# Phase 1 of a bidirectional RWKV-7 and short-convolution layer: TensorE's order written out by hand in the recurrence's groups

## The chip, the cores and the metric

The kernel runs on one core of one Trainium2 chip. The metric is the device time of one execution in microseconds (us). The time given for a kernel is the median of its runs; before the change it is 1721.12 us (three runs, 1720.58 to 1724.52).

## What is computed

One layer on 2176 tokens (128 context tokens, then 2048 latent tokens in rows of 64) of width 1024. Cut to what matters here (the heads are 64 wide, `d` is the direction of the scan):

```python
h = rmsnorm(x) * (1 + scale) + shift
r, k, v, g_a, b_gate, c_gate, u_conv, g_b = split(h @ w_in)      # 8 x 512 columns
r, k, v = token_shift(r, k, v)                                   # neighbours in a row, mixed by mu
w[d] = w0[d] + tanh(h @ decay_down[d]) @ decay_up[d]             # "lora": 64 wide
decay[d] = exp(-exp(-softplus(-w[d]) - 0.5))
a[d] = sigmoid(iclr_bias[d] + (h @ iclr_down[d]) @ iclr_up[d])
kk = k * kk_scale;  kk = kk / norm_per_head(kk)
kd[d] = k * (1 + (a[d] - 1) * ka_scale)
y = scan(r, decay, kd, v, kk, a, both directions)                # phase 2
y = groupnorm(y) + sum_per_head(r * (kd[0] + kd[1]) * bonus_rk) * v
ya = y * silu(g_a);  yb = b_gate * conv3(c_gate * u_conv) * silu(g_b)
out = x + gate * (concat(ya, yb) @ w_out);  out = rmsnorm(out)
```

## The kernel before

Three phases follow each other. Phase 1 makes the projections and everything that the scan needs and spills it to scratch in HBM; phase 2 does the scan in chunks; phase 3 does the output projection. The change is in phase 1.

Phase 1 goes over the tokens in three thirds of two blocks each (`THIRD`, `BLK`): five blocks have 384 tokens, the last has 256. In a third the blocks' inputs `h` stay in SBUF. First `lora_down` projects both blocks onto the loras (four tiles `mml`, in PSUM). Then come the recurrence's groups: for each of four groups `g` of 128 channels and each block `j` of the third, `groupA(g, j, ...)`, which I call a unit, so eight units to a third. Then `groupB` does the convolution's groups in the same manner (`mmc`, `mmu`, `mmgb`, `mmb`).

`dense` is one projection of one unit, 24 matmuls of 128x128 by 384 columns (8 slices of the width, times three products of high and low parts, lines 158 to 160). In the order in which the program is written a unit is:

- `mmk`, the keys. `shifted` takes them from PSUM with two ScalarE operations (`rawl`, `q1k`), GpSimd adds the neighbours (`shk`, line 314), VectorE joins them (`ok`, line 320). ScalarE squares them (`sq`), and `part_sum` sums the squares per head: `parts_of` splits a tile into a high part (ScalarE, `hshs`, line 194) and a low part (GpSimd, `hsls`, line 195), and two matmuls with a matrix of ones sum both (`pss`, lines 202 and 203).
- `mmr`, the receptances, shifted alike (`or`).
- For each direction the two lora-ups (`up`, lines 355 and 356, eight matmuls to a unit), a tanh of each (ScalarE `t` and `ta`), a scan over the chunk (VectorE, lines 365 and 367), exponentials (`pp`), and four operands for phase 2, written on VectorE into a ring of four `sp` tiles and spilled (`al`, `rh`, `ka`, `be`, lines 377 to 392).
- The bonus: `kd` of both directions are added (line 396) and multiplied by `rS` (line 397; I call its result `bs`), and `part_sum` sums it per head: ScalarE `hshb`, GpSimd `hslb`, TensorE `psb`.
- `mmv`, the values, shifted (`ov`), transposed by three matmuls (`psv`, line 403), freed of their mean (`vmean`, `vt`, lines 412 and 413) and spilled from `vt` by a DMA on SP's queue (line 414).
- `mmg`, the gate (`sg`), and last `q`, which needs `psb`, `ov` and `sg`, spilled like the operands.

Three things bind these steps to each other. PSUM has five buffers for the projections and lora-ups (`pmm`) and three for the sums and transposes (`pax`). The low parts of both sums and the transposed values share one SBUF buffer: `lo` in `parts_of` and `vt` both have the tag `"vt"` with `bufs=1`, so the next low part can only be written when the values have left the buffer by their DMA. The high parts share one too (`"hsh"`), and the squares `sq` share theirs with `lf` of `lora_down`.

The order of the instructions on each engine is not the written one: a list scheduler with a timing model of its own sets it when the program is built, on all engines in phase 1. On the chip each engine then runs its list strictly in that order. (Phase 2 already has its main part under `tc.manual_schedule`, which keeps the written order on the engines that it names.) On TensorE the scheduler starts each unit before the one ahead is finished: `psb` and `psv` of a unit stand between the products of the next one.

Of the kernel before, what the change touches and what calls it, by code (L numbers as in the profile page):

```python
# [10 lines left out]
ALU = mybir.AluOpType  # L11
# [38 lines left out]
def phase1(K):  # L50
# [50 lines left out]
    def dcol(i):  # L101
        return dv[:, i:i + 1]
# [48 lines left out]
    def dense(w, hh, n, nm):  # L151
        ps = pmm.tile([128, 384], F32, tag="mm", name=f"mm{nm}_{K.u()}")
        products(ps, w, hh, n, range(8))
        return ps
# [43 lines left out]
    def part_sum(o, t_, n, nm, eng=G):  # L198

        hi, lo = parts_of(t_, n, nm, eng)  # L200
        ps = pax.tile([128, 384], F32, tag="ax", name=f"ps{nm}")
        T.matmul(ps[:, :n], o[:], hi[:, :n], start=True, stop=False)
        T.matmul(ps[:, :n], o[:], lo[:, :n], start=False, stop=True)
        return ps
# [123 lines left out]
    def groupA(g, j, ws, hh, lw, pre):  # L328
        t0, n = BLK[j]
# [2 lines left out]
        wk, wr_, wv, wg = ws  # L332
        psk, psr = pre or (None, None)

        kS = shifted(psk or dense(wk, hh, n, "k"), j, 1, g, "k", 1)
        sq = tl("sq")
        P.activation(sq[:, :n], kS[:, :n], AF.Square, scale=vcol(V_KK + g))
        pss = part_sum(onr, sq, n, f"s{g}_{j}")
# [4 lines left out]
        P.activation(kk[:, :n], kS[:, :n], AF.Identity, scale=vcol(V_KK + g))  # L343
        kkn = n2
        V.tensor_tensor(kkn[:, :n], kk[:, :n], n2[:, :n], ALU.mult)
        rS = shifted(psr or dense(wr_, hh, n, "r"), j, 0, g, "r", 1)
        kds = []
        for d in range(2):
            cs = slice(g * 128, g * 128 + 128)
# [45 lines left out]
        bs = kds[0]  # L395
        V.tensor_tensor(bs[:, :n], kds[0][:, :n], kds[1][:, :n], ALU.add)
        V.scalar_tensor_tensor(bs[:, :n], bs[:, :n], dcol(D_RKQ + g), rS[:, :n], ALU.mult, ALU.mult)
        psb = part_sum(onr, bs, n, f"b{g}_{j}")
        vS = shifted(dense(wv, hh, n, "v"), j, 2, g, "v", 1)

        psv = pax.tile([128, 3, 128], F32, tag="ax", name=f"psv{g}_{j}")
        for i in range(n // 128):
            T.transpose(psv[:, i, :], vS[:, i * 128:(i + 1) * 128], idt[:])
# [9 lines left out]
        V.scalar_tensor_tensor(heads(vt), mn[:, :m].unsqueeze(3).broadcast_to((128, m, 2, 64)), -1.0 / 64, heads(psv), ALU.mult, ALU.add)  # L413
        nc.sync.dma_start(S["vt"][t0:t0 + n, g * 128:(g + 1) * 128].rearrange("(a p) c -> p a c", p=128), vt[:, :n // 128])

        psg = dense(wg, hh, n, "g")
        tg = tl("sg", 2)
        P.activation(tg[:, :n], psg[:, :n], AF.Tanh, scale=0.5)
        sg = tg
        V.scalar_tensor_tensor(sg[:, :n], tg[:, :n], 1.0, psg[:, :n], ALU.add, ALU.mult)  # L420
        spill("sg", g, j, sg, "sg")
        q = tl("sp", 4)
        V.tensor_tensor(q[:, :n], psb[:, :n], vS[:, :n], ALU.mult)
        V.scalar_tensor_tensor(q[:, :n], q[:, :n], dcol(D_GBH + g), sg[:, :n], ALU.add, ALU.mult)
        spill("q", g, j, q, "q")

    def groupB(g, j, ws, hh):
        t0, n = BLK[j]
# [92 lines left out]


    up = {}

    def run(gen):
        for _ in gen:
# [17 lines left out]
    for t3, js in enumerate(THIRD):  # L544
        wd, wi = wlora if t3 == 0 else (load_w(32), load_w(33))
        lws = {}
        pre = {}
        for j in js:
            if j not in hs:
                if t3 == 0:  # L550
                    pre[0] = psf[2:]
                    ws = ws0 + [load_w(cb) for cb in (8, 12)]
                    nc.sync.dma_start(smask[:], A["cst"][:, 128:512])
                run(make_h(j, xb[j]))
            lws[j] = lora_down(j, wd, wi, psf[:2] if j == 0 else None)
        if t3 == 0:
            load_up()
        for g in range(4):
            if t3 or g:
                ws = [load_w(cb + g) for cb in (4, 0, 8, 12)]  # L560
            for j in js:
                groupA(g, j, ws, hs[j], lws[j], pre.pop(j, None))
        early = gate_rows() if t3 == 0 else iter(())
        if t3 == 2:
            for p in (pax, ta_, hr, ca):
                p.close()
            early = K.early()
        for g in range(4):
            ws = [load_w(cb + g) for cb in (20, 24, 28, 16)]
            for j in js:  # L570
                groupB(g, j, ws, hs[j])
                for _ in range(4 if t3 == 2 else 1):
                    next(early, None)
            if g == 1 and t3 < 2:
                j, j2 = THIRD[t3 + 1]
                run(make_h(j, norm(j, load_x(j))))
                xb[j2] = norm(j2, load_x(j2))
        for _ in early:
            pass
# [925 lines left out]
```

## Time and profile before

| | |
|---|---|
| median of three runs | 1721.12 us |
| the profiled execution | 1714.66 us, its span 1712.9 us |
| TensorE's mean granted clock | 0.957 |
| recurrence's groups, third 1 | 69.9 to 236.2 us of the span: 166.3 us |
| recurrence's groups, third 2 | 406.7 to 585.9 us: 179.2 us |
| recurrence's groups, third 3 | 736.9 to 880.3 us: 143.4 us |
| phase 2's first products | from 907.8 us |

The windows begin where TensorE has done the lora-downs and end where it begins the convolution's groups. Times of single rows are microseconds from the start of the span; a matmul's own duration is longer than the distance to the next, since they are pipelined, so a string of matmuls is measured from start to start. `[x <-Y]` behind a row of the timeline is the time that the engine stood idle ahead of it, and what ended that.

### The profile page before, as it was taken

Reading aid. Unit: us, or ns where it says so; the run is one execution under the profiler, and the core shown is the slowest. Engines: PE = TensorE matmul, PEld = TensorE weight load, DVE = VectorE, ACT = ScalarE, POOL = GpSimd, SP = SyncE. Lnnn points to the kernel's source line nnn. Section 1 sums busy time; section 2 is a strip of 40 time slices with the busy share of each in tenths; the row PEclk is TensorE's granted clock in tenths of the full one; section 3 lists DMA queues with packets and bytes.
Section 4 is the critical chain, followed back from the end, with each engine's and each line's share of the span. In section 5 each row is a group of like instructions: output and inputs, shape, how many; then the busy total and the mean of one; then the engine's idle time right before and its main releaser. Section 6 shows DMA issues by size and latency. Waiting matters only on the chain. (4 is left out here: it accounts for less than half of the span.)

```text
span 1712.9 us, 42020 instructions
## 1 busy us (share of the span) xinstructions
PE 1561.0 (91%) x17364; PEld 1432.1 (84%) x17364; DVE 1145.1 (67%) x2133; ACT 792.4 (46%) x1590; POOL 517.4 (30%) x951
## 2 busy tenths in 40 slices
PE   5999899999888999999999988888989898898998
PEld 2898899899788999989898987778878786776886
DVE  5988887544677736466884455788888885475333
ACT  4555554323444413145541135777768676422222
POOL 0022220000222200012214406676767675121221
PEclk7999999999999999999999988999999998799999
DMA  9688876674788835448876644556575744454342
GB/s 373 219 246 236 241 235 226 224 244 117 194 199 192 195 127 182 161 128 222 228 205 225 235 101 131 147 143 183 145 186 154 179 132 136 128 180 162 119 147 92
DMA packets 204271, 313.43 MB, mean 183 GB/s; under 512 B 58024, under 2 KB 147496, under 8 KB 190000
## 3 DMA queue, kind: packets, MB, share of 16 engines
q1 hardware_dynamic: 168496, 310.61, 60.0%
q10 hardware_dynamic: 35584, 0.14, 1.4%
q8 instruction: 136, 2.23, 0.6%
q14 instruction: 55, 0.45, 0.1%
HBM read 207.79 MB, written 102.91 MB: 181 GB/s over the span
## 5 line engine op out<-in xcount | busy, mean ns | idle before, releaser
L912 POOL TENSOR_TENSOR zt<-zt,ztmp 128x30 f32<-128x30 f32 (+7 forms) x510 | 201.6, 395 | 39.7
L909 POOL TENSOR_TENSOR ztmp<-ab,zt 128x60 f32<-128x60 f32 (+7 forms) x255 | 134.2, 526 | 129.5 <-DVE ab L900 110.9
L1048 PE MATMUL psS<-sv,E 128*64 128x64 f32 x2176 | 105.4, 233 | 16.3 <-DVE sv L1074 10.2
L1048 PEld LDWEIGHTS psS<-sv,E 128*64 128x64 f32 x2176 | 90.8, 144 | 31.4 <-issue 16.0
L314 POOL TENSOR_TENSOR shk<-rawl 128x384 f32<-128x384 f32 (+1 forms) x24 | 20.5, 854 | 276.8 <-ACT rawl L310 276.7
L1074 DVE TENSOR_TENSOR sv<-psS,pc 64x128 f32<-64x128 f32 x254 | 66.6, 278 | 55.3 <-PE psS L1048 54.0
L1022 DVE TENSOR_TENSOR E<-psE,msk 128x512 f32<-128x512 f32 x136 | 91.5, 680 | 17.5 <-PE psE L1017 16.8
L1003 ACT ACTIVATE stf<-psX 64x512 f32<-64x512 f32 x136 | 80.4, 591 | 32.9 <-PE psX L999 31.0
L158 PE MATMUL mmv<-h,w 128*128 128x384 f32 (+1 forms) x192 | 70.2, 366 | 19.7 <-ACT q1r L312 10.6
L1441 POOL TENSOR_TENSOR z<-z,x 128x512 f32<-128x512 f32 x32 | 41.1, 1288 | 149.8 <-DVE z L1437 121.1
L999 PE MATMUL psX<-F,zb 64*64 64x128 f32 x1088 | 52.0, 302 | 19.8 <-issue 11.8
L159 PE MATMUL mmv<-h,w 128*128 128x384 f32 (+1 forms) x192 | 68.1, 354 | 0.0
L160 PE MATMUL mmv<-h,w 128*128 128x384 f32 (+1 forms) x192 | 67.7, 353 | 0.1
L158 PE MATMUL mmg<-h,w 128*128 128x384 f32 (+1 forms) x192 | 63.4, 330 | 3.3 <-ACT rawc L317 1.6
L158 PE MATMUL mmc<-h,w 128*128 128x384 f32 (+1 forms) x192 | 64.2, 335 | 0.5 <-DMA w<-scr_wsp 0.5
L159 PE MATMUL mmc<-h,w 128*128 128x384 f32 (+1 forms) x192 | 63.1, 329 | 0.0
L158 PE MATMUL mmgb<-h,w 128*128 128x384 f32 (+1 forms) x192 | 63.1, 328 | 0.0
L160 PE MATMUL mmc<-h,w 128*128 128x384 f32 (+1 forms) x192 | 63.0, 328 | 0.0
L160 PE MATMUL mmb<-h,w 128*128 128x384 f32 (+1 forms) x192 | 62.9, 328 | 0.0
L159 PE MATMUL mmgb<-h,w 128*128 128x384 f32 (+1 forms) x192 | 62.9, 328 | 0.0
L195 POOL TENSOR_TENSOR hsls<-sq,hshs 128x384 fp32r<-128x384 f32 (+1 forms) x24 | 30.6, 1277 | 106.8 <-DMA scr_vt<-vt 41.9
L160 PE MATMUL mmgb<-h,w 128*128 128x384 f32 (+1 forms) x192 | 62.9, 327 | 0.0
(312 smaller groups left out, 5147.0 us busy)
## 6 DMA issues: line engine op xcount, KB each, us to landing
w<-scr_wsp SPq DMA_DIRECT2D x68, 1024.0 KB, 6.6
scr_wsp<-w SPq DMA_DIRECT2D x34, 1024.0 KB, 6.1
rr<-scr_ops SPq DMA_DIRECT2D x32, 1024.0 KB, 9.0
scr_ops<-sp SPq DMA_DIRECT2D x160, 192.0 KB, 5.3
wr<-in_win SPq DMA_DIRECT2D x34, 512.0 KB, 7.4
x<-in_x SPq DMA_DIRECT2D x17, 512.0 KB, 3.7
wadas<-in_wada SPq DMA_DIRECT2D x8, 1024.0 KB, 15.0
sv<-scr_vt SPq DMA_DIRECT2D x32, 256.0 KB, 3.7
```

The lines of the kernel that those rows point to most:

```text
L158: T.matmul(ps[:, :n], w[:, 0, k], hh[:, 0, k, :n], start=k == 0, stop=False)
L159: T.matmul(ps[:, :n], w[:, 0, k], hh[:, 1, k, :n], start=False, stop=False)
L160: T.matmul(ps[:, :n], w[:, 1, k], hh[:, 0, k, :n], start=False, stop=k == 7)
L195: eng.tensor_tensor(lo[:, :n], t_[:, :n], hi[:, :n].bitcast(F32), ALU.subtract)
L909: G.tensor_tensor(tv, ab[:, j:j + 2, j + 2:32].unsqueeze(1).broadcast_to((128, kn, 2, n)), zt[:, :kn, j:j + 2].unsqueeze(3).broadcast_to(( ...
L912: G.tensor_tensor(zt[:, :kn, j + 2:32], zt[:, :kn, j + 2:32], tv[:, :, r], ALU.subtract)
L999: T.matmul(px[e][hr_, a, :], B.zb[er, gi * 8 + hd * 4 + a, :], g.F[er, hd * 4 + a, :], start=True, stop=True)
L1003: P.activation(g.fs[64:128, :, hd, e::2], g.ps["X"][e][hr_].rearrange("p a (b t) -> p b a t", b=2), AF.Copy, scale=-1.0)
L1022: V.tensor_tensor(g.E[n][:, k:k + 2].rearrange("p a b c -> p (a b) c"), pe[:].rearrange("p a b c -> p (a b) c"), B.msk[:, ME[g.d]].unsquee ...
L1048: T.matmul(g.sp[i // 4][r, q, hd, :], g.E[n][:, k, hd, r], g.sv[:, u, hd, :], start=True, stop=True)
L1074: V.tensor_tensor(dst, g.sp[i // 4][0:64, q], B.pc[0:64, d, 2 * p:2 * p + 2, c:c + 1].broadcast_to((64, 2, 64)), ALU.mult)
L1441: (V if last else G).tensor_tensor(z[:, cs], z[:, cs], xt[:, cs], ALU.add)
```

## The change

TensorE is put under `manual_schedule` for the recurrence's groups, so it keeps the written order there, and the written order is changed. The other engines' orders are still the scheduler's. In the new order a unit is `mmk`, then the bonus sum `psb` of the unit before (held in `later`), `mmr`, `pss`, `mmv`, the eight lora-ups, `mmg`, `psv`. The bonus of a third's last unit is summed after the manual stretch. The number of matmuls, operations and DMAs is unchanged.

```diff
-        kS = shifted(psk or dense(wk, hh, n, "k"), j, 1, g, "k", 1)
+        psk = psk or dense(wk, hh, n, "k")
+        for f in later:
+            f()
+        later.clear()
+        kS = shifted(psk, j, 1, g, "k", 1)
+        psr = psr or dense(wr_, hh, n, "r")
         sq = tl("sq")
...
-        rS = shifted(psr or dense(wr_, hh, n, "r"), j, 0, g, "r", 1)
+        rS = shifted(psr, j, 0, g, "r", 1)
+        vS = shifted(dense(wv, hh, n, "v"), j, 2, g, "v", 1)
...
-        psb = part_sum(onr, bs, n, f"b{g}_{j}")
-        vS = shifted(dense(wv, hh, n, "v"), j, 2, g, "v", 1)
-
+        psg = dense(wg, hh, n, "g")
         psv = pax.tile([128, 3, 128], F32, tag="ax", name=f"psv{g}_{j}")
...
-        psg = dense(wg, hh, n, "g")
...
-        q = tl("sp", 4)
-        V.tensor_tensor(q[:, :n], psb[:, :n], vS[:, :n], ALU.mult)
-        V.scalar_tensor_tensor(q[:, :n], q[:, :n], dcol(D_GBH + g), sg[:, :n], ALU.add, ALU.mult)
-        spill("q", g, j, q, "q")
+        def bonus():
+            psb = part_sum(onr, bs, n, f"b{g}_{j}")
+            q = tl("sp", 4)
+            V.tensor_tensor(q[:, :n], psb[:, :n], vS[:, :n], ALU.mult)
+            V.scalar_tensor_tensor(q[:, :n], q[:, :n], dcol(D_GBH + g), sg[:, :n], ALU.add, ALU.mult)
+            spill("q", g, j, q, "q")
+
+        later.append(bonus)
...
+        order = tc.manual_schedule(engines={mybir.EngineType.PE})
+        order.__enter__()
         for g in range(4):
...
                 groupA(g, j, ws, hs[j], lws[j], pre.pop(j, None))
+        order.__exit__(None, None, None)
+        for f in later:
+            f()
+        later.clear()
```

On TensorE, the place in the second third where the bonus of unit (1, 3), that is `g` 1 and block 3, is summed while unit (2, 2) runs. Before, it stands among the lora-ups of the next unit, behind that unit's `mmk` and `mmr`:

```order
L160 MATMUL mmr_581_4768<-h2_3006,w2_572_4716 128x384
L355 MATMUL up0_585_4800<-lw0_2_3649,ups_601 128x384
L356 MATMUL up0_585_4800<-lw0_2_3649,ups_601 128x384
L355 MATMUL up1_587_4809<-lw2_2_3651,ups_601 128x384
L356 MATMUL up1_587_4809<-lw2_2_3651,ups_601 128x384
L202 MATMUL psb1_3_4637<-hshb1_3_4633,onr_103 128x384
L403 MATMUL psv1_3_4672<-idt_94,ov_567_4670 128x128 x3
L355 MATMUL up0_594_4831<-lw1_2_3650,ups_601 128x384
L356 MATMUL up0_594_4831<-lw1_2_3650,ups_601 128x384
L355 MATMUL up1_596_4840<-lw3_2_3652,ups_601 128x384
L203 MATMUL psb1_3_4637<-hslb1_3_4634,onr_103 128x384
L356 MATMUL up1_596_4840<-lw3_2_3652,ups_601 128x384
```

and with the change both of its matmuls stand between the next unit's `mmk` and `mmr`:

```order
L158 MATMUL mmk_574_4716<-h2_3009,w6_570_4708 128x384
L159 MATMUL mmk_574_4716<-h2_3009,w6_570_4708 128x384
L160 MATMUL mmk_574_4716<-h2_3009,w6_570_4708 128x384
L202 MATMUL psb1_3_4745<-hshb1_3_4741,onr_103 128x384
L203 MATMUL psb1_3_4745<-hslb1_3_4742,onr_103 128x384
L158 MATMUL mmr_579_4759<-h2_3009,w2_571_4710 128x384
L159 MATMUL mmr_579_4759<-h2_3009,w2_571_4710 128x384
L160 MATMUL mmr_579_4759<-h2_3009,w2_571_4710 128x384
```

So the sum moved up by 24 matmuls of `mmr` and four to eight lora-ups, and the whole of `mmr` now stands behind it.

On VectorE, unit (2, 2) from its first scan to `bs`, the operation whose result the bonus sum is made of (`t` scans, `kd` the keys of a direction, `sp` operands: `kk` goes into `al`, `or` into `rh`, `t` into `ka`). Before:

```order
L365 SCALAR_TENSOR_TENSOR t_2_2_586_4803<-smask_107,t_2_2_586_4803 128x384
L386 TENSOR_TENSOR kd_2_2_591_4821<-kd_2_2_591_4821,ok_578_4752 128x384
L367 SCALAR_TENSOR_TENSOR t_2_2_595_4834<-smask_107,t_2_2_595_4834 128x384
L386 TENSOR_TENSOR kd_2_2_600_4852<-kd_2_2_600_4852,ok_578_4752 128x384
L377 TENSOR_TENSOR sp_2_2_589_4814<-kk_2_2_580_4765,pp0_0_473 128x384
L380 TENSOR_TENSOR sp_2_2_590_4817<-or_584_4798,pp0_0_473 128x384
L388 TENSOR_TENSOR sp_2_2_592_4824<-kd_2_2_591_4821,t_2_2_586_4803 128x384
L396 TENSOR_TENSOR kd_2_2_591_4821<-kd_2_2_591_4821,kd_2_2_600_4852 128x384
L397 SCALAR_TENSOR_TENSOR kd_2_2_591_4821<-kd_2_2_591_4821,dv_114,or_584_4798 128x384
```

With the change the same four operations (two scans, two `kd`) come first, and then:

```order
L383 TENSOR_TENSOR sp_2_2_593_4851<-kk_2_2_581_4795,pp0_0_473 128x384
L386 TENSOR_TENSOR sp_2_2_594_4854<-or_584_4803,pp0_0_473 128x384
L416 TENSOR_REDUCE vmean2_2_4931<-psv2_2_4926 128x6
L423 SCALAR_TENSOR_TENSOR sg_2_2_608_4935<-sg_2_2_608_4935,mmg_607_4901 128x384
L394 TENSOR_TENSOR sp_2_2_596_4861<-kd_2_2_595_4858,t_2_2_590_4840 128x384
L397 SCALAR_TENSOR_TENSOR sp_2_2_597_4864<-ta_2_2_592_4849,sq_2_2_580_4784 128x384
L417 SCALAR_TENSOR_TENSOR vt2_2_4930<-vmean2_2_4931,psv2_2_4926 128x384
L383 TENSOR_TENSOR sp_2_2_602_4882<-kk_2_2_581_4795,pp1_0_474 128x384
L402 TENSOR_TENSOR kd_2_2_595_4858<-kd_2_2_595_4858,kd_2_2_604_4889 128x384
L398 TENSOR_TENSOR sp_2_2_597_4864<-sp_2_2_597_4864,t_2_2_590_4840 128x384
L386 TENSOR_TENSOR sp_2_2_603_4885<-or_584_4803,pp1_0_474 128x384
L403 SCALAR_TENSOR_TENSOR kd_2_2_595_4858<-kd_2_2_595_4858,dv_114,or_584_4803 128x384
```

Nine operations ahead of and with `bs` have become sixteen: `vmean`, the gate, `vt`, one `be` (two operations) and the second direction's `al` and `rh` moved ahead of it. The reciprocal of the keys' norm, which stood behind `bs` here, now stands ahead of the first scan.

On ScalarE at the start of the first third, the squares of unit (0, 0)'s keys, whose sum `pss` now stands on TensorE right behind the lora-downs. Before, unit (0, 0)'s lora-ups, values and gate run on TensorE meanwhile, and their evictions stand between the last lora-down's eviction `lf` and the split of the squares:

```order
L536 ACTIVATE lf1_1_592<-mml1_18_567 128x384
L371 ACTIVATE t_0_0_28_641<-t_0_0_28_641,nln2_110 128x384
L382 DMA scr_pc0_58<-pp0_0_473 128x6x1
L370 ACTIVATE pp1_0_474<-t_0_0_37_672 128x6x64
L310 COPY rawl0_464<-mmv_45_709 128x4x64
L312 ACTIVATE q1v_46_735<-mmv_45_709,dv_114 128x384
L317 COPY rawc0_466<-mmv_45_709 128x128
L371 ACTIVATE t_0_0_37_672<-t_0_0_37_672,nln2_110 128x384
L382 DMA scr_pc1_60<-pp1_0_474 128x6x1
L337 ACTIVATE sq_0_0_22_615<-ok_21_613,vec_99 128x384
L418 ACTIVATE sg_0_0_50_778<-mmg_49_753 128x384
L194 CAST hshs0_0_617<-sq_0_0_22_615 128x384
```

With the change the squares come right behind `lf`:

```order
L545 ACTIVATE lf0_1_561<-mml0_17_536 128x384
L545 ACTIVATE lf1_1_592<-mml1_18_567 128x384
L342 ACTIVATE sq_0_0_22_617<-ok_21_615,vec_99 128x384
L194 CAST hshs0_0_619<-sq_0_0_22_617 128x384
```

They still come after it, since `sq` takes over the buffer of `lf`. What moved on TensorE is that `pss` of this unit now stands ahead of its values and lora-ups, where before `mmv`, the lora-ups, `mmg`, and the next unit's `mmk` and the start of its `mmr` stood ahead of it.

More of the change, by code (lines that the diff above doesn't have):

```diff
@@ L523, in phase1 @@
     up = {}
+    later = []
     def run(gen):
```

## Prediction

> **What bounds the kernel now.** I read the page's busy shares first, then the busy time by stage, TensorE's waits, and the timeline of one unit. Two rows of busy time on the page, then the three windows of the recurrence's groups:
>
> ```profile
> PE 1561.0 (91%) x17364; PEld 1432.1 (84%) x17364; DVE 1145.1 (67%) x2133; ACT 792.4 (46%) x1590; POOL 517.4 (30%) x951
> ...
> 69.90:236.20 166.30, 152.76 (x835) 149.36 (x835) 148.89 (x221) 100.34 (x198) 41.59 (x36) 0.96 0.82 244
> ...
> 406.70:585.90 179.20, 160.16 (x886) 155.44 (x885) 131.91 (x203) 89.37 (x183) 40.92 (x39) 0.97 0.77 179
> 736.90:880.30 143.40, 135.12 (x881) 132.02 (x880) 109.13 (x193) 79.16 (x175) 34.38 (x38) 0.96 0.74 198
> ```
>
> The columns behind a window's length are TensorE's matmuls, its weight loads, VectorE, ScalarE, GpSimd, the granted clock and DMA. TensorE is the bound, VectorE close behind it (149 of 166 us in the first third). The change acts only here, in 166.3 + 179.2 + 143.4 = 488.9 us.
>
> What TensorE needs without waits comes from its own strings of matmuls, start to start:
>
> ```profile
> 494.87 0.33 PE L158 MATMUL mmk<-h,w 128*128 128x384 f32 x1
> ...
> 499.03 0.33 PE L158 MATMUL mmr<-h,w 128*128 128x384 f32 x1
> ...
> 503.19 0.34 PE L355 MATMUL up<-lw,ups 128*128 128x384 f32 x1
> ...
> 506.29 0.49 PE L403 MATMUL psv<-idt,ov 128*128 128x128 f32 x3
> ...
> 772.11 0.28 PE L159 MATMUL mmv<-h,w 128*128 128x256 f32 x1
> 772.23 0.28 PE L160 MATMUL mmv<-h,w 128*128 128x256 f32 x1
> ```
>
> A projection of 384 columns takes 4.16 us (24 matmuls at 0.173). A unit is 4 x 4.16 + 12 more matmuls (2.1) + the transposes (0.4) = 19.1 us; with 256 columns, at 0.12, 108 x 0.12 + 0.27 = 13.2. The first third has 8 x 19.1, less the two projections (8.3) that unit (0, 0) gets ready-made and one bonus sum that falls behind it (0.3): 144.2. The second 152.5, the third 4 x 19.1 + 4 x 13.2 - 0.2 = 129.0. Together 425.7, so 63 us are waits and slow stretches now. The two largest of these waits over the run:
>
> ```profile
> PE psb L202 <- ACT hshb L194: 14.0, 8, 2.7
> ...
> PE mmv L158 <- ACT q1r L312: 10.6, 6, 3.3
> ```
>
> A perfect order could win 63 us at most.
>
> **The change, part by part.** Nothing is added or taken away, so the price is in what TensorE waits for. Three places.
>
> *The bonus sum in each unit.* `psb` of unit X now stands behind the next unit's `mmk`. Between the end of X's `mmv` and it TensorE has eight lora-ups (1.4), `mmg` (4.16), `psv` (0.4) and `mmk` (4.16) to do, with the first sum's matmul (0.17) 10.3 us. In these `bs`, its high part and its low part must be made. These rows give the chain:
>
> ```profile
> 509.05 0.46 ACT L310 COPY rawl<-mmr 128x384 f32<-128x384 f32 x1
> ...
> 509.88 0.58 ACT L361 ACTIVATE t<-up,dv 128x384 f32<-128x384 f32 x1
> ...
> 512.57 0.95 DVE L365 TENSOR_TENSOR_SCAN t<-smask,t 128x384 f32<-128x384 f32 x1
> ...
> 516.03 0.55 DVE L377 TENSOR_TENSOR sp<-kk,pp 128x384 f32<-128x384 f32 x1
> ...
> 516.50 0.55 DVE L380 TENSOR_TENSOR sp<-or,pp 128x384 f32<-128x384 f32 x1
> ...
> 518.77 0.62 DVE L397 SCALAR_TENSOR_TENSOR kd<-kd,dv,or 128x384 f32<-128x384 f32 x1
> ...
> 519.48 0.51 ACT L194 CAST hshb<-kd 128x384 fp32r<-128x384 f32 x1 [2.18 <-DVE kd L397]
> ...
> 520.06 1.19 POOL L195 TENSOR_TENSOR hslb<-kd,hshb 128x384 fp32r<-128x384 f32 x1 [2.34 <-ACT hshb L194]
> ...
> 531.06 0.58 ACT L361 ACTIVATE t<-up,dv 128x384 f32<-128x384 f32 x1
> ...
> 533.59 0.96 DVE L365 TENSOR_TENSOR_SCAN t<-smask,t 128x384 f32<-128x384 f32 x1 [1.35 <-ACT t L362]
> ```
>
> ScalarE first evicts `mmv`, as it does `mmr` here: 0.1 + 0.83 (509.05 to 509.88), then the tanh steps up to the scan, in the order of the second unit shown, which is also the new one: 2.53 (531.06 to 533.59). That is 3.46. VectorE takes 3.46 for the two scans and two `kd` (512.57 to 516.03), then 0.47 for each operation (516.03 to 516.50). The orders set out above have nine of these ahead of `bs` in one kind of unit, eleven in the other; ten make 4.7, `bs` itself 0.62, together 8.8. From the end of `bs` to the end of the low part, 519.39 to 521.25, is 1.86. The chain is 3.46 + 8.8 + 1.86 = 14.1 us against 10.3 of cover: TensorE waits 3.8 us in every unit, and `mmr`, `pss` and `mmv` of the next unit, everything behind it, wait too. VectorE's reciprocal doesn't lengthen this: it falls behind `pss`, while `mmv` runs.
>
> *The shared buffer.* The low part of X's bonus is written where `vt` of X stands, and VectorE makes `vt` ahead of `bs`. Such a wait is seen in before, for the other sum's low part:
>
> ```profile
> 511.55 0.37 SPq L414 DMA_DIRECT2D scr_vt<-vt  x1
> ...
> 514.05 1.64 POOL L195 TENSOR_TENSOR hsls<-sq,hshs 128x384 fp32r<-128x384 f32 x1 [3.64 <-DVE kd L386]
> ...
> scr_vt<-vt SPq DMA_DIRECT2D x20, 192.0 KB, 5.1
> ```
>
> `vt` is done 3.46 + 3.46 + 6 x 0.47 + 0.55 = 10.3 us behind `mmv`; the low part could start at 12.9. A DMA that lands in 2.5 us (511.55 to 514.05) costs nothing more, the median one of 5.1 costs 2.5. In one unit of two the next group's weights, 1 MB each, are loaded at that time and share the DMA engines with it, so I take half, 1.3.
>
> *Slow stretches.* After a wait the array often issues at half speed:
>
> ```profile
> 158.82 0.69 PE L158 MATMUL mmv<-h,w 128*128 128x384 f32 x1 [3.91 <-ACT rawc L317]
> 159.31 0.52 PE L159 MATMUL mmv<-h,w 128*128 128x384 f32 x1
> 159.63 0.52 PE L160 MATMUL mmv<-h,w 128*128 128x384 f32 x1
> ...
> 510.04 0.44 PE L158 MATMUL mmv<-h,w 128*128 128x384 f32 x1 [2.32 <-ACT q1r L312]
> 510.32 0.34 PE L159 MATMUL mmv<-h,w 128*128 128x384 f32 x1
> 510.50 0.35 PE L160 MATMUL mmv<-h,w 128*128 128x384 f32 x1
> ```
>
> After 3.91 us it went on at 0.32 us a matmul for sixteen matmuls (0.145 too long each, 2.3 us lost), after 2.32 us at 0.18 at once. Between 0 and 2.3 I take 1.6, nearer the longer wait. A unit thus loses 3.8 + 1.3 + 1.6 = 6.7 us, seven times in a third, since the first has no bonus before it. On this the Trainium skill ("TensorE: Matmul & The Clock Gate", Part 1) says that the clock halves only after a whole idle window of about 3.4 us. Here each wait is cut by the high part's matmul into pieces of some 2 to 3 us, so by that rule alone no stretch would be slow, and the sum would be 21 x 1.6 = 34 us smaller. The row that bears on it is the one at 158.82; the one at 510.04 agrees with the rule too.
>
> *The start.* `pss` of unit (0, 0) now stands right behind the lora-downs, and its squares behind the last `lf`:
>
> ```profile
> 69.73 0.34 PE L160 MATMUL mml<-h,w 128*128 128x384 f32 x1
> ...
> 74.33 0.73 DVE L540 CAST lw<-lf 64x384 fp32r<-64x384 f32 x2
> ...
> 76.08 1.14 DVE L541 TENSOR_TENSOR lw<-lf,lw 64x384 fp32r<-64x384 f32 x2
> ...
> 77.25 0.49 ACT L536 ACTIVATE lf<-mml 128x384 f32<-128x384 f32 x1 [0.62 <-DVE lw L541]
> ...
> 83.25 0.62 ACT L337 ACTIVATE sq<-ok,vec 128x384 f32<-128x384 f32 x1 [2.60 <-DVE lw L541]
> ...
> 84.73 1.01 POOL L195 TENSOR_TENSOR hsls<-sq,hshs 128x384 fp32r<-128x384 f32 x1 [4.20 <-ACT hshs L194]
> ```
>
> Without the scan that ran between 74.33 and 76.08, `lf` comes at 76.2, then 0.49 + 0.73 + 1.14 for it and its two splits, 0.62 for the squares, 0.5 and 1.0 for their parts: 80.9. TensorE, done at 69.9, waits 11 us there, where it now does lora-ups, values and gate; with a slow stretch of 2.3, 13.3.
>
> **The sum.** Second third: 152.5 + 7 x 6.7 = 199.4, against 179.2: +20. First third: VectorE and ScalarE also split weights there, a cast in front of the tanh and a subtraction in front of `bs`:
>
> ```profile
> L127 ACT CAST w<-wr x34: 1033/1048/1062, 20.3 to 358.1; 128x1024 fp32r<-128x1024 f32 x34
> ...
> L128 DVE TENSOR_TENSOR w<-wr,w x34: 1153/1217/2064, 21.7 to 359.4; 128x1024 fp32r<-128x1024 f32 x34
> ```
>
> That is 2.3 us more in the units of the second block; in those of the first `vt` stands behind `bs`, so its DMA adds about as much. 144.2 + 13.3 + 7 x 9.0 = 220.5, against 166.3: +54. Third third: behind the four units of 384 columns stands a `mmk` of 256, 1.3 us less cover, and one more VectorE operation and a half than the ten counted (0.9): 4 x 8.9; the three of 256 have a chain about a quarter shorter, and a `mmk` of 384 to hide it: I take 2.7 each. 129.0 + 35.6 + 8.1 = 172.7, against 143.4: +29. Together +103 us. The profiled execution took 1714.66, so 1818; the median of the runs is 6.5 us above it, so 1824. Behind these windows nothing changes: the convolution's groups and phase 2 only begin later.
>
> **The rivals.** *It gets faster.* If the chain fits behind the lora-ups, `mmg` and `mmk`, TensorE runs through: all 63 us but the start's 13 are won, 1671. That turns on one length: a gain begins where a unit loses under (63 - 13) / 21 = 2.4 us. Against it stands the quoted unit, which from its scan to the end of the low part took 512.57 to 521.25 = 8.7 us with seven operations fewer ahead of `bs`, and with the 3.46 in front 12.1, still over 10.3. For it: the reciprocal is out of the way, and VectorE has more slack.
>
> *Half as bad.* Every `vt` lands in 2.5 us and slow stretches are short (0.8): 4.6 us lost in a unit; 152.5 + 32, 144.2 + 12 + 7 x 5.7, 129 + 32.5 = 542, +53: 1774.
>
> *VectorE is the bound either way.* Its work is unchanged, and with 149 of 166 us in the first third a new order on TensorE would only move the waits: no change, 1721. Against it: in the second third it is busy 132 of 179.
>
> *The queue chokes.* Operands wait for the ring of four `sp` tiles in front of `bs`, and each `vt` lands in 5.1 us or more. With 10 us lost in a unit of the second third, 12 in the other units of 384 columns and 5 in those of 256, the windows are 222, 242 and 192: +167, 1888. For it: DMA is 0.74 to 0.82 busy there.
>
> **How the numbers follow.** My forecast 0.67, half as bad 0.15, the choked queue 0.07, faster 0.08, no change 0.03. The range goes from a little below half as bad to the choked queue: 1762 to 1888. Within 0.3% (5 us), about what a measurement of this kernel can tell from no change, I put 0.03; faster 0.08, slower 0.89.
>
> **What would show it.** Right: TensorE's waits led by `psb` on `hshb` and on `hslb`, some 4 to 5 us together in nearly every unit, `hslb` waiting for `scr_vt<-vt`; a first wait of about 11 us for `pss` at 70; the waits of `mmv` for `q1r` gone; windows of about 220, 199 and 173 us. Wrong: if `bs` begins within 9 us of the end of `mmv`, or `psb` hardly waits, the length of VectorE's chain was misjudged; if the waits are there but the windows no longer, TensorE wasn't the bound.

## The result, and the profile after

The changed kernel takes 1935.64 us (median of four runs, 1930.34 to 1941.98) beside 1720.85 us for the kernel before on the same chip: ratio 1.1253, 95% interval 1.1198 to 1.1307. It is slower, and by twice what was forecast: +215 us instead of +103.

Busy time of the whole execution from the page after, and the three windows of the recurrence's groups (columns as before):

```profile
PE 1600.1 (83%) x17364; PEld 1465.8 (76%) x17364; DVE 1134.3 (59%) x2133; ACT 792.2 (41%) x1590; POOL 511.8 (27%) x951
...
69.50:318.20 248.70, 165.26 (x842) 158.89 (x840) 150.03 (x233) 103.36 (x205) 43.59 (x37) 0.81 0.66 168
487.30:724.20 236.90, 170.87 (x885) 165.68 (x884) 128.62 (x202) 89.58 (x180) 39.18 (x39) 0.84 0.60 136
880.50:1097.20 216.70, 150.87 (x883) 146.02 (x882) 112.86 (x202) 79.22 (x179) 30.61 (x39) 0.81 0.58 140
```

The windows now last 702.3 us, against 488.9: +213.4, nearly the whole loss. VectorE, ScalarE and GpSimd have nearly the same busy time in them as before (within 4 us); only TensorE's grew, from 448.0 to 487.0 us for the same matmuls, at a granted clock of 0.81 to 0.84 where it was 0.96 to 0.97. Outside the windows the span holds 1226.0 us, before 1224.0; of its stretches only the one between the second and the third window is longer (156.3 us, before 151.0).

TensorE's waits over the run (total, times, longest):

```profile
PE psb L202 <- ACT hshb L194: 113.4, 21, 10.6
PE psb L203 <- POOL hslb L195: 98.8, 24, 9.7
...
PE pss L202 <- ACT hshs L194: 9.1, 1, 9.1
```

The two matmuls of the bonus sum lead, as forecast, and the wait of `mmv` for `q1r` is gone. In the windows alone `psb` waits 205 us and `pss` 10.3. With the 425.7 us of work without waits this makes 641; the other 61 us are what is left for slow stretches and small gaps.

What ends these waits differs from unit to unit. Two places of the second third, from the timeline: first, `psb` of a unit of the second block; then, `psb` of a unit of the first.

```profile
604.38 0.69 SPq L418 DMA_DIRECT2D scr_vt<-vt  x1
...
606.54 0.44 PE L202 MATMUL psb<-hshb,onr 128*128 128x384 f32 x1 [1.51 <-ACT hshb L194]
...
614.07 1.26 POOL L195 TENSOR_TENSOR hslb<-kd,hshb 128x384 fp32r<-128x384 f32 x1 [7.55 <-DMA scr_vt<-vt]
615.38 0.69 PE L203 MATMUL psb<-hslb,onr 128*128 128x384 f32 x1 [8.39 <-POOL hslb L195]
...
640.66 0.56 DVE L383 TENSOR_TENSOR sp<-kk,pp 128x384 f32<-128x384 f32 x1 [4.92 <-DMA scr_ops<-sp]
643.19 0.51 ACT L194 CAST hshb<-kd 128x384 fp32r<-128x384 f32 x1 [5.69 <-DVE kd L403]
643.76 0.69 PE L202 MATMUL psb<-hshb,onr 128*128 128x384 f32 x1 [7.31 <-ACT hshb L194]
645.53 0.69 PE L203 MATMUL psb<-hslb,onr 128*128 128x384 f32 x1 [1.09 <-POOL hslb L195]
```

In the second block's unit the high part is nearly in time (1.51 us), but `vt` leaves the shared buffer only 9.7 us after its DMA was issued (604.38 to 614.07). In the first block's unit the buffer is free, but VectorE, four operations ahead of `bs`, waited 4.92 us until the ring of `sp` tiles had a free one (`al`, line 383). Both are transfers. Over the run VectorE waits 132.5 us at that line, 24 times (in one unit of two ahead of `bs`, in the other behind it), and GpSimd 170.9 us for `vt`:

```profile
DVE sp L383 <- DMA scr_ops<-sp: 132.5, 24, 6.7
...
POOL hslb L195 <- DMA scr_vt<-vt: 170.9, 18, 18.8
...
scr_ops<-sp SPq DMA_DIRECT2D x160, 192.0 KB, 6.1
...
scr_vt<-vt SPq DMA_DIRECT2D x20, 192.0 KB, 6.9
```

And behind the wait, `mmr` of the next unit runs at half speed:

```profile
581.55 0.69 PE L202 MATMUL psb<-hshb,onr 128*128 128x384 f32 x1 [7.08 <-ACT hshb L194]
...
583.33 0.69 PE L203 MATMUL psb<-hslb,onr 128*128 128x384 f32 x1 [1.09 <-POOL hslb L195]
...
583.82 0.52 PE L158 MATMUL mmr<-h,w 128*128 128x384 f32 x1
...
584.14 0.52 PE L159 MATMUL mmr<-h,w 128*128 128x384 f32 x1
...
588.62 0.34 PE L158 MATMUL mmr<-h,w 128*128 128x384 f32 x1
...
588.79 0.34 PE L159 MATMUL mmr<-h,w 128*128 128x384 f32 x1
```

Matmuls start 0.32 us apart until 588.62 and 0.17 apart from there: 15 of them 0.15 us too late each, 2.2 us, for a wait that was over at 583.33. The two matmuls of the sum itself are slow too: from 581.55 to the next `pss` at 590.20 it takes 8.65 us, of which 1.09 are wait and 26 x 0.173 = 4.5 the matmuls at full speed, so some 3.1 us are lost.

### The profile page after: what moved, and what is told of

Read it like the earlier page. It is cut to its first block, busy times and chain, and to the rows that moved or that the text cites. A ratio compares the mean times of both kernels' runs of the same rounds, so it can differ in the third digit from the quotient of the medians.

```text
span 1928.3 us, 42037 instructions
## 1 busy us (share of the span) xinstructions
PE 1600.1 (83%) x17364; PEld 1465.8 (76%) x17364; DVE 1134.3 (59%) x2133; ACT 792.2 (41%) x1590; POOL 511.8 (27%) x951
## 4 chain that ended last, share of the span: by engine, by line
PE 51%; DMA 16%; issue 13%; DVE 11%; ACT 4%; POOL 3%; SPq 1%; DVEq 0%; POOLq 0%; ACTq 0%
DMA scr_vt<-vt 7%; PE psE L1032 5%; DMA scr_ops<-sp 4%; PE psu L1393 3%; PE psu L1395 3%; PE psS L1063 3%; PE psu L1394 3%; PE mmr L158 2%; PE mmr L159 2%; PE mmr L160 2%; PE psFm L855 2%; PE psX L1014 2%; POOL hslb L195 2%; PE mmv L160 1%; PE mmv L158 1%
## 5 line engine op out<-in xcount | busy, mean ns | idle before, releaser
L1063 PE MATMUL psS<-sv,E 128*64 128x64 f32 x2176 | 106.7, 235 | 18.2 <-DVE sv L1089 12.7
L1063 PEld LDWEIGHTS psS<-sv,E 128*64 128x64 f32 x2176 | 91.9, 146 | 35.4 <-DVE sv L1089 14.5
L202 PE MATMUL psb<-hshb,onr 128*128 128x384 f32 (+1 forms) x24 | 13.7, 573 | 113.4 <-ACT hshb L194 113.4
L383 DVE TENSOR_TENSOR sp<-kk,pp 128x384 f32<-128x384 f32 (+1 forms) x48 | 25.6, 533 | 132.5 <-DMA scr_ops<-sp 132.5
L203 PE MATMUL psb<-hslb,onr 128*128 128x384 f32 (+1 forms) x24 | 15.6, 651 | 98.8 <-POOL hslb L195 98.8
L202 PEld LDWEIGHTS psb<-hshb,onr 128*128 128x128 f32 x24 | 6.0, 250 | 119.6 <-ACT hshb L194 119.6
L203 PEld LDWEIGHTS psb<-hslb,onr 128*128 128x128 f32 x24 | 6.7, 279 | 107.1 <-POOL hslb L195 107.1
L195 POOL TENSOR_TENSOR hslb<-kd,hshb 128x384 fp32r<-128x384 f32 (+1 forms) x24 | 31.8, 1324 | 203.5 <-DMA scr_vt<-vt 170.9
L158 PE MATMUL mmr<-h,w 128*128 128x384 f32 (+1 forms) x184 | 77.3, 420 | 0.0
L159 PE MATMUL mmr<-h,w 128*128 128x384 f32 (+1 forms) x184 | 76.3, 415 | 0.0
L160 PE MATMUL mmr<-h,w 128*128 128x384 f32 (+1 forms) x184 | 74.9, 407 | 0.0
L459 ACT ACTIVATE sg<-mmgb 128x384 f32<-128x384 f32 (+1 forms) x24 | 11.4, 473 | 132.3 <-PE mmgb L160 132.3
L158 PE MATMUL mmc<-h,w 128*128 128x384 f32 (+1 forms) x192 | 63.9, 333 | 0.0
L160 PE MATMUL mmgb<-h,w 128*128 128x384 f32 (+1 forms) x192 | 63.5, 331 | 0.0
```

The lines of the kernel that those rows point to most:

```text
L158: T.matmul(ps[:, :n], w[:, 0, k], hh[:, 0, k, :n], start=k == 0, stop=False)
L159: T.matmul(ps[:, :n], w[:, 0, k], hh[:, 1, k, :n], start=False, stop=False)
L160: T.matmul(ps[:, :n], w[:, 1, k], hh[:, 0, k, :n], start=False, stop=k == 7)
L195: eng.tensor_tensor(lo[:, :n], t_[:, :n], hi[:, :n].bitcast(F32), ALU.subtract)
L1063: T.matmul(g.sp[i // 4][r, q, hd, :], g.E[n][:, k, hd, r], g.sv[:, u, hd, :], start=True, stop=True)
```

## The experiments

Theory: the fixed place of `psb` puts the chain (evict the values, scans, `kd`, `bs`) on TensorE's path; two transfers, that of `vt` out of the shared buffer and those of the operands out of the ring, lengthen it; and each wait is paid a second time at half speed. Rivals: one of the transfers alone, the written order as such, or a low clock that has nothing to do with the waits.

These kernels ran beside the kernel before on three other chips, where that took 1703 to 1706 us, so they are compared by ratios. Windows are summed over the three thirds; before 488.9, after 702.3. They are microseconds of one profiled execution, and the kernel before was profiled on the first chip only. On the others it takes 15 to 18 us less, and no trace shows in which stage, so a difference of windows of that size against 488.9 says little by itself.

The scheduler also lays the other engines' lists anew for each kernel. In the second third VectorE's is nearly that of the changed kernel with the own buffer, the fillers and the other queue; with the ring, the later place and the kernels before it is another.

| kernel | ratio [95%] | windows, us | TensorE busy in them |
|---|---|---|---|
| after | 1.1253 [1.1198, 1.1307] | 702.3 | 487.0 |
| own buffer | 1.1133 [1.1071, 1.1196] | 662.5 | 499.0 |
| ring of eight | 1.1222 [1.1164, 1.1280] | 683.6 | 489.8 |
| both | 1.0700 [1.0665, 1.0735] | 594.9 | 483.8 |
| order left to the scheduler | 1.0178 [1.0145, 1.0210] | 486.5 | 451.3 |
| late place | 1.0991 [1.0931, 1.1051] | 647.0 | 485.9 |
| late place and both | 1.0251 [1.0207, 1.0296] | 524.5 | 461.0 |
| 32 fillers | 1.1449 [1.1382, 1.1516] | 705.8 | 564.0 with fillers |
| 64 fillers | 1.1391 [1.1361, 1.1421] | 682.3 | 616.8 with fillers |
| `vt` on ScalarE's queue | 1.1264 [1.1227, 1.1301] | 696.3 | 491.3 |
| before, ring of eight | 0.9918 [0.9884, 0.9953] | 462.7 | 438.6 |
| before, both | 0.9844 [0.9822, 0.9866] | 461.5 | 436.3 |

**The shared buffer.** The bonus's low part gets a buffer of its own.

```diff
-        lo = ta_.tile([128, 384], F32R, tag="vt", name=f"hsl{nm}", bufs=1)
+        lo = ta_.tile([128, 384], F32R, tag="vt" if nm[0] != "b" else "lob", name=f"hsl{nm}", bufs=1)
```

> The change, with the bonus's low part in an SBUF buffer of its own, so that it no longer waits until the transposed values have left the shared one. Theory T (the loss beyond the prediction is waits for transfers: vt's DMA in the units of the second block, the ring of operand tiles in those of the first): psb's waits on hslb fall from 92 us in the three windows to about 25, but in the second block's units ok still stands behind al, which waits for its tile, so pss takes some 2 us back there; net -45 us, about 1890. Rival R (VectorE's list of operations and the half-speed stretches are longer than predicted, transfers are hidden behind them): -10 us at most, above 1920.

Measured: 1893.55 us, but beside a before of 1702.96: ratio 1.1133, that is 1916 us by the first chip's measure, between the two expectations. TensorE's waits:

```profile
PE psb L202 <- ACT hshb L194: 106.9, 21, 9.9
PE pss L202 <- ACT hshs L194: 37.7, 10, 9.2
PE psb L203 <- POOL hslb L195: 11.9, 21, 1.1
```

`hslb` is 87 us lighter, but `pss` now waits 37.7 instead of 9.1, and `hshb` keeps its 107. The buffer alone is worth a tenth of the loss by the ratio, and 40 of the 213 us in the windows.

**The ring.** Eight operand tiles, in the buffer of `x`, which is idle there (`rh`, `ka`, `be` and `q` take theirs from it likewise).

```diff
-            al = tl("sp", 4)
+            al = spt()
...
+        spx = ta_.tile([128, 8, 384], F32, tag="x", name=f"spx{t3}", bufs=1)
+        spr[:] = [spx[:, i] for i in range(8)]
```

> The change, with eight operand tiles in the ring instead of four (they lie in the buffer of x, which is idle in these windows). T: VectorE's waits for scr_ops<-sp, 116 us in the three windows, go; psb's wait on hshb in units of the first block falls from 7.3 to about 3.5 us, while the wait on hslb for vt's DMA in those of the second stays at 8 to 9; -45 us, about 1890. R: less than 10 us.

Measured: ratio 1.1222, not to be told from the changed kernel. VectorE's waits for the ring are gone, and `psb` waits less for `hshb`, 83.0 us instead of 113.4. Yet GpSimd waits for `vt`, and TensorE behind it, as long as before:

```profile
PE psb L203 <- POOL hslb L195: 104.4, 23, 6.8
PE psb L202 <- ACT hshb L194: 83.0, 21, 5.4
...
POOL hslb L195 <- DMA scr_vt<-vt: 177.8, 24, 19.4
```

But this edit does more than free the ring. With eight tiles the scheduler puts more of the second direction's operands ahead of `bs`, and in the second third also the next unit's `ok`: 18 operations from the first scan to `bs` in every unit there, where the changed kernel has 14 or 16. The rows are the first scan and `bs`, first in the changed kernel, in a unit that doesn't wait for the ring, then with the ring of eight and the own buffer; the ring alone has nearly the same list:

```profile
534.70 0.96 DVE L371 TENSOR_TENSOR_SCAN t<-smask,t 128x384 f32<-128x384 f32 x1 [1.35 <-ACT t L368]
...
541.55 0.61 DVE L403 SCALAR_TENSOR_TENSOR kd<-kd,dv,or 128x384 f32<-128x384 f32 x1
...
521.10 0.96 DVE L371 TENSOR_TENSOR_SCAN t<-smask,t 128x384 f32<-128x384 f32 x1
...
530.16 0.62 DVE L320 SCALAR_TENSOR_TENSOR ok<-shk,dv,q1k 128x384 f32<-128x384 f32 x1 [0.72 <-POOL shk L314]
530.69 0.61 DVE L403 SCALAR_TENSOR_TENSOR kd<-kd,dv,or 128x384 f32<-128x384 f32 x1
```

In the changed kernel `bs` starts 6.85 us behind the first scan in units of the second block, and 12.6 to 13.3 in those of the first, which wait for the ring; with eight tiles it is 9.6 in every unit of this third. So `bs` comes some 3 us earlier in one unit of two, where it finds the buffer still taken, and 2.7 us later in the other. The small gain is thus not the ring's wait alone.

**Both together.**

> The change with both, a buffer of its own and eight operand tiles. T: what is left is the chain that the prediction counted, 3.8 us of wait and 1 to 1.5 more since the scheduler now puts al and rh of both directions ahead of bs, and 2.5 of slow stretch in a unit: windows of about 606 us together instead of 702, 1840. Only here are both waits gone, so it falls by at least as much as e1 and e2 together. R: above 1900.

Measured: ratio 1.0700, 1841 us by the first chip's measure. 1.2% and 0.3% alone became 5.5% together, and 107 of the 213 us in the windows are gone. Freeing the buffer is worth 683.6 - 594.9 = 88.7 us where VectorE doesn't wait for the ring, and 702.3 - 662.5 = 39.8 where it does; within each of these pairs VectorE's list is nearly the same. So the ring's wait hides a good part of the buffer's. What stays is regular. Two units of the second third, and the sum over the windows (their length, then busy times):

```profile
505.32 0.69 PE L202 MATMUL psb<-hshb,onr 128*128 128x384 f32 x1 [4.58 <-ACT hshb L194]
506.39 0.69 PE L203 MATMUL psb<-hslb,onr 128*128 128x384 f32 x1 [0.39 <-POOL hslb L195]
506.88 0.52 PE L158 MATMUL mmr<-h,w 128*128 128x384 f32 x1
...
532.38 0.69 PE L202 MATMUL psb<-hshb,onr 128*128 128x384 f32 x1 [4.60 <-ACT hshb L194]
...
sum 594.90, PE 483.78 PEld 466.88 DVE 383.46 ACT 269.91 POOL 120.21; mean PE 161.26 PEld 155.62 DVE 127.82 ACT 89.97 POOL 40.07
```

In the second third every unit takes 27.0 to 27.3 us, 8.0 or a little more above its 19.1 of work: 5.0 wait for the chain, here with VectorE's longer list, and the matmuls behind them lose the other 3 at half speed.

**The order.** The new written order stays, but the manual schedule goes, so the scheduler orders TensorE again.

```diff
-        order = tc.manual_schedule(engines={mybir.EngineType.PE})
-        order.__enter__()
...
-        order.__exit__(None, None, None)
```

> The change without the manual schedule: the new written order (values ahead of the lora-ups, bonus behind the next keys) but TensorE's list made by the scheduler as before. If the fixed order on TensorE is the cause: 1721 within 15 us, and psb no longer leads the waits. If the new written order alone makes it slow: above 1760.

Measured: ratio 1.0178, 1752 us by the first chip's measure, 16 beyond the expected band and short of the rival's 1760; `psb` no longer leads (12.7 and 4.1 us over the run). The windows are back at their length of before:

```profile
sum 486.50, PE 451.30 PEld 437.96 DVE 377.76 ACT 266.04 POOL 105.25; mean PE 150.43 PEld 145.99 DVE 125.92 ACT 88.68 POOL 35.08
```

So nearly all of the loss comes from TensorE's fixed order, not from the written order as such. Whether the written order costs the 1.8%, some 30 us, stays open. Against the profile of the first chip 18 us of them stand behind the last window: from there to the end it takes 850.5 us, before 832.6. That part is unchanged in the program; why it is longer was not found. Among the other kernels here it takes 828 to 849.

**A later place.** The bonus is summed behind the next unit's values, so that `mmr`, `pss` and `mmv` cover it too.

```diff
-        for f in later:
-            f()
-        later.clear()
...
-        vS = shifted(dense(wv, hh, n, "v"), j, 2, g, "v", 1)
+        psv_ = dense(wv, hh, n, "v")
+        for f in later:
+            f()
+        later.clear()
+        vS = shifted(psv_, j, 2, g, "v", 1)
```

> The changed kernel with one move: the bonus is summed behind the next unit's values instead of behind its keys, so TensorE has mmk, mmr, pss and mmv (about 10 us more) between the gates and psb. Nothing else differs. The theory (the head sum stands too early for the chain scan, al, kd, bs and for the transfer of vt): the waits psb<-hshb (113 us) fall under 20 us, but hsls of the next unit now stands in the vt buffer ahead of hslb, so a part of the vt wait comes back at pss<-hsls: 20 to 60 us. Windows 425.7 + 60 + 25 = 510 us, ratio 1.02 (1.00 to 1.05). The rival (the loss comes from the chain itself being longer than a unit, or from written order as such, and a later place only moves the wait to the next instruction): the waits of psb move to mmv, mmw or pss with the same sum, ratio 1.09 or more.

Measured: ratio 1.0991, a miss. The waits at `psb` are down to 5.3 us, as the theory has it, but most of them came back at `pss`, where I had 20 to 60 us. The row of waits, and one unit's keys in the timeline:

```profile
PE pss L202 <- ACT hshs L194: 150.8, 22, 10.7
...
578.86 0.82 POOL L314 TENSOR_TENSOR shk<-rawl 128x384 f32<-128x384 f32 x1 [9.66 <-ACT rawl L310]
...
587.29 0.61 DVE L320 SCALAR_TENSOR_TENSOR ok<-shk,dv,q1k 128x384 f32<-128x384 f32 x1
...
589.88 0.69 PE L202 MATMUL pss<-hshs,onr 128*128 128x384 f32 x1 [7.46 <-ACT hshs L194]
```

It isn't `vt` that holds `pss` up. The shifted keys are there at 579.7, but VectorE joins them only at 587.29: in its own order that stands behind the operands of the unit before, and these wait for the ring (117.8 us at `al` in this run). So the chain now reaches TensorE through the next unit's keys, which is the rival's reading: a later place mostly moves the wait.

> The same late place, with a buffer of its own for the low parts and a ring of eight operand tiles in the idle x buffer, so that neither transfer is waited for. The theory: hardly a wait is left in the three windows, and half-speed stretches go with them: 425.7 + 10 to 40 us against the 488.9 of the kernel before, start wait of 9 us included: ratio 0.985 (0.97 to 1.00), the version that may beat both. The rival (written order costs by itself, as the 1.8 per cent of the free order hint): 1.01 to 1.03.

Measured, with the late place, a buffer apart from `vt` for the low parts of both sums, and the ring together: ratio 1.0251, a miss, inside the rival's 1.01 to 1.03. `psb` waits 0.2 us in the whole run, `pss` still 51.5:

```profile
PE pss L202 <- ACT hshs L194: 51.5, 20, 9.0
...
sum 524.50, PE 460.97 PEld 447.21 DVE 394.41 ACT 267.90 POOL 107.05; mean PE 153.66 PEld 149.07 DVE 131.47 ACT 89.30 POOL 35.68
```

The best fixed order tried remains 36 us in the windows behind the scheduler's, which puts other units' matmuls in front of both sums. What of this is the written order's cost, as the rival has it, no run separates.

**The same relief for the kernel before.**

> The kernel before with only the ring of eight operand tiles. Before, VectorE waits some 55 us at al for the ring in the three windows, while TensorE waits little. The theory (the ring counts only where TensorE's next instruction hangs on the chain behind it): no difference, ratio 1.000 (0.993 to 1.004), with VectorE's waits at al gone. The rival (the ring's waits are a cost of their own in any order): 0.98 or less.

> The kernel before with the ring of eight operand tiles and a buffer of its own for the bonus's low part. The ring alone gave 0.992 (0.988 to 0.995). Before, hardly anything waits for the vt buffer on TensorE's path, so I expect no more than the ring gives: 0.992 (0.985 to 0.996). The rival (in the kernel before the vt buffer too was hidden only by the ring's wait, as in the changed kernel): 0.985 or less.

Measured: 0.9918 and 0.9844. Both are faster than the kernel before, and both are misses of mine on the low side; the second meets the rival's figure of 0.985 or less. The ratio puts the ring of eight at 0.8%, 14 us of the whole. The windows are 26 us shorter than in the first chip's profile, which is more than the ratio bears out. With the buffer too, their sum is the same, though thirds differ by up to 10 us each way:

```profile
sum 462.70, PE 438.61 PEld 428.73 DVE 388.10 ACT 268.15 POOL 118.18; mean PE 146.20 PEld 142.91 DVE 129.37 ACT 89.38 POOL 39.39
...
sum 461.50, PE 436.32 PEld 426.98 DVE 391.06 ACT 269.75 POOL 117.93; mean PE 145.44 PEld 142.33 DVE 130.35 ACT 89.92 POOL 39.31
```

The first row is the ring alone, the second both. The scheduler makes a new order on all engines for them, TensorE included, so this isn't the ring's wait alone. The two ran on different chips; their profiles differ behind the last window (839 and 828 us), where the program is the same, so I don't put the further 0.7% down to the buffer. That the rival has it right is not excluded.

**Is half speed made by the waits?** Matmuls of `onr` by `onr` into `psb`, ahead of the bonus's two, which overwrite them, keep the array busy while it would wait.

```diff
+        for i in range(64 if nm[0] == "b" else 0):
+            T.matmul(ps[:, :128], o[:], o[:], start=True, stop=True)
```

> The changed kernel with 32 matmuls of onr by onr (128x128, some 0.15 to 0.25 us each, 5 to 8 us a unit) written into psb ahead of the bonus's two matmuls; their result is overwritten. They fill a part of the 9 to 10 us that TensorE waits there. The theory that the waits cost a second time, through half speed behind them (some 62 us over the unwaited work): the granted clock in the windows rises from 0.81 to 0.84 to above 0.90, mmr behind psb takes 4.2 us and not up to 6.4, and the kernel gets faster although TensorE has more to do: ratio 1.105 (1.09 to 1.12). The rival (the low clock has another cause than the waits): the clock stays near 0.82, and the ratio stays at 1.125 or rises.

Measured with 32: ratio 1.1449, a miss. They took 3.7 us instead of 5 to 8, so that waits of up to 6.9 us stayed behind them. The clock rose in the second and third window only (0.82, 0.90 and 0.87), and the first grew by 14 us, which I can't explain. Without the fillers, 21 x 3.68 = 77 us in the windows, TensorE's busy time there is 486.7, as it was (the 476 of the next expectation takes off all 24 fillings, of which three fall behind the windows). Inconclusive, so once more with 64:

> The filler run again with 64 matmuls of onr by onr ahead of the bonus's two instead of 32, since 32 took only 3.7 us a unit and left waits of 3 to 7 us behind them. 64 take 7.4 us, about what psb waits in a unit in sum. The theory that waits are paid a second time at half speed: the waits of psb fall from 127 to some 50 us, the clock in the windows rises above 0.92, TensorE's busy time there without the fillers falls from 476 to about 450 us, and the windows fall to about 425.7 + 177 of fillers + 60 + 20 = 685 us, against 702 without fillers and 706 with 32: ratio 1.12 to 1.135. The rival (fillers are simply added, the clock is not made by the waits): windows 740 us or more, TensorE's own busy time unchanged, ratio 1.16.

Measured: the timeline of one unit, then the three windows.

```profile
580.15 7.25 PE L203 MATMUL psb<-onr 128*128 128x128 f32 x64
...
587.30 0.44 PE L204 MATMUL psb<-hshb,onr 128*128 128x384 f32 x1
588.60 0.44 PE L205 MATMUL psb<-hslb,onr 128*128 128x384 f32 x1 [0.86 <-POOL hslb L195]
588.88 0.34 PE L158 MATMUL mmr<-h,w 128*128 128x384 f32 x1
589.05 0.34 PE L159 MATMUL mmr<-h,w 128*128 128x384 f32 x1
...
69.50:313.10 243.60, 211.90 (x1285) 208.40 (x1286) 150.55 (x232) 103.01 (x205) 42.62 (x37) 0.92 0.64 172
493.40:723.30 229.90, 214.21 (x1333) 211.52 (x1332) 129.34 (x202) 89.71 (x180) 37.95 (x39) 0.96 0.59 140
884.60:1093.40 208.80, 190.67 (x1329) 187.71 (x1329) 112.94 (x202) 79.22 (x180) 30.65 (x39) 0.93 0.59 146
```

`mmr` starts 0.17 us apart at once, the clock is 0.92 to 0.96, and the windows are 20 us shorter than without fillers (14 us against the 696.3 of the other queue, which ran on the same chip) although TensorE does 21 x 7.25 = 152 us more in them. Without those its busy time is 616.8 - 152 = 464.5, against 487.0. That the idle waits bring most of the slow stretches is thereby shown. The ratio, 1.1391, still lies above the expected 1.12 to 1.135: three of the 24 fillings fall behind the windows (up to 22 us), and another 11 us outside are not accounted for.

**The queue of `vt`.** Its DMA is issued by ScalarE instead of SyncE.

```diff
-        nc.sync.dma_start(S["vt"][t0:t0 + n, ...
+        nc.scalar.dma_start(S["vt"][t0:t0 + n, ...
```

> The changed kernel with the DMA of vt issued by ScalarE instead of SyncE, so that it does not stand in one queue behind weight loads of 1 MB and operand spills; ScalarE pays its issue, 0.4 to 0.7 us a unit. If vt lands 7 to 10 us after its issue because of what stands ahead of it in that queue, it lands in 3 to 5, GpSimd's hslb waits 40 to 70 us for it instead of 121, psb<-hslb 60 instead of 99, and the ratio comes near that of the run with a buffer of its own, 1.113. The rival (the sixteen engines serve all queues by turns, so it is their load that sets the landing): landing and waits as they were, ratio 1.12 to 1.13.

Measured: ratio 1.1264, no change; the rival holds.

```profile
scr_vt<-vt ACTq DMA_DIRECT2D x20, 192.0 KB, 6.1
```

From issue to landing it is 6.1 us, by SyncE's queue 6.9; `psb` still waits 93 us for `hslb`. What stands ahead in that queue accounts for 0.8 us of the landing at most. The Trainium skill fits this ("Trainium Kernel Development and Optimization", Key Constraints): DMAs of all these queues run on the same sixteen engines, and issuing from several saves only the time to issue. This run agrees.

## Why the prediction was wrong, point by point

The direction, the place and the chain's wait were right, and the size was half. The step that failed is the wait for transfers: one was put at 1.3 us a unit, the other, for the ring, at nothing. In the second third a unit loses (236.9 - 152.5) / 7 = 12.1 us instead of 6.7. By an estimate from the two units shown, the chain is about 3.0 of them, the transfers 6.1 on the mean (7.3 for `vt` in one kind of unit, 4.9 for the ring in the other), and the slow stretches the remaining 3.

- *The chain.* Forecast 14.1 us against 10.3 of cover, 3.8 of wait a unit. In the changed kernel, less the ring's 4.92, the first block's unit waits 7.31 + 1.09 - 4.92 = 3.5 us, and the second block's, with the low part 1.09 behind the high part, 1.51 + 1.09 = 2.6: about 3.0, so 3.8 was a little too much. One reason: the 3.46 us for the two scans and two `kd` were read off rows of which one `kd` took 1.30 us instead of 0.53; in the changed kernel's unit shown above the four take 2.6 (534.70 to 537.34). The 5.0 us of "both together" belong to a VectorE list longer by two to four operations and a wait of 0.7.
- *The shared buffer.* This term failed: 1.3 us a unit, taken between a landing in 2.5 and one in 5.1 us, durations read from the kernel before. In the changed kernel the median landing is 6.9, in the unit shown it is 9.7, and TensorE waits 8.39 us there where 1.09 would do, 7.3 too long. `vt`, operands and weights go out in the same few microseconds there; that this crowd delays the landing is likely, but no run tests it.
- *The ring.* It is in the sum nowhere: VectorE's chain was added up from operations that run back to back. I put the ring's waits into one rival only, "the queue chokes", with a chance of 0.07, although TensorE's order was about to put VectorE's `al` on the path. VectorE waits 4.9 us there in the unit shown, 132.5 / 24 = 5.5 on the mean. With both transfers taken away 107 of the 213 us go, although VectorE's list ahead of `bs` is longer then; so they probably cost more, and how much more no run shows. Alone, the buffer gives 1.2% and the ring's edit 0.3%. That rival had the right mechanism; its 1888 was still 48 us too low, with 10 us lost in a unit of the second third where 12.1 were.
- *Slow stretches.* Forecast 1.6 us a unit, from waits of 2 to 3 us. Waits came as 7.1 + 1.1 or 1.5 + 8.4, and even 4.6 + 0.4 cost 3 us. Beside the work and the waits the windows hold 61 us, where the forecast's slow stretches sum to 36; TensorE's busy time for the same matmuls rose from 448.0 to 487.0. The Trainium skill's rule that I weighed ("TensorE: Matmul & The Clock Gate", Part 1: half speed after a whole idle window of about 3.4 us, full again after as long a busy one) was right in its first half, and my premise that the waits stay below it was wrong: the trace has 7.08 us idle, then half speed. The way back took longer than that here, 5.3 us behind the wait that ended at 583.33.
- *The start.* Forecast 11 us for `pss` of the first unit; measured 9.1 + 0.4.
- *By thirds* the forecast was 220, 199 and 173, measured 248.7, 236.9 and 216.7; with both transfers taken away 211.3, 209.7 and 173.9. That this sum, 594.9, is close to the forecast 592.6 is chance: it holds no wait for `vt`, which the forecast had, but a longer VectorE list and larger slow stretches, which it had not.
- *The signs* named as right were there for the waits: `psb` led them, `hslb` waited for `scr_vt<-vt`, `q1r` was gone. They were there at twice the size, 9 to 10 us in a unit for the 4 to 5 forecast, and the windows had not the lengths named. Neither sign of being wrong came: `bs` began at 541.55 in the unit shown, some 10 us behind the last matmul of its `mmv` at 530.93, and the windows grew with the waits.

## What to carry to other kernels

When an in-order engine is made to wait for a chain, walk that chain for waits on transfers too, such as a ring of output tiles or a buffer shared with something spilled: what was slack on a side engine becomes part of the path, at the landing times of the new crowd, not of the old trace. Two such waits in parallel can hide each other, so taking one away shows little (1.2% and 0.3% here); take both away before judging. When a scheduler lays the other engines, look at their lists again after each edit, since an edit that frees a wait may also move work in front of it. And price an idle stretch of TensorE of 5 to 10 us, as they were here, at its length and 2 to 3 us more.

## What I had not expected of the hardware

What half speed adds behind a wait hardly grows with the wait. From the first matmul of the bonus sum to the next `pss`, less the wait between its two matmuls and 4.5 us of matmuls at full speed, 2.8 us are lost behind 4.6 + 0.4 us of wait (505.32 to 513.00, both transfers away), 3.1 behind 7.1 + 1.1 (581.55 to 590.20) and 2.2 behind 1.5 + 8.4 (606.54 to 621.65). Useless matmuls ahead of a wait made the windows 14 to 20 us shorter, though in total that kernel was no faster. In the kernel before, where VectorE waited 66 us for the ring over the run (28.1 + 20.7 + 14.5 + 2.2 + 0.4 at five lines) and TensorE's own waits looked small, a ring of eight operand tiles instead of four still made the whole 0.8% shorter. And all that stands behind the last window (the last third's convolution groups, phases 2 and 3), with the same work in every kernel, took 828 to 851 us: differences of a per cent in the whole time are not all the change's own.
